# Scores of attention group B as two 128-row products and a set of four 32-row products, with the PSUM banks dealt out by hand and the second projections moved ahead of the output projection

## The chip, the cores and the metric

The kernel runs on one core of a Trainium2 chip. The metric is the time of one execution in microseconds (us) on the device. Three runs of the kernel before gave 1156.81, 1157.28 and 1157.65 us; their median, 1157.28 us, is the time before. The engines are named as in the profile: PE multiplies matrices and writes into PSUM, an accumulator of eight banks of 128 x 512 floats; PEld loads PE's stationary operand; DVE, ACT and POOL work on vectors; SP issues most of the DMAs.

## The reference

The program is two layers of an encoder over 512 tokens of width 1024. Only the first layer's attention matters here. It has two head groups: A, eight heads with grouped keys, and B, eight heads of latent attention. For B:

```python
qb = (rmsnorm(cq, b_q_norm) @ b_w_uq).reshape(b, s, B_HEADS, B_NOPE + B_ROPE)      # 64 + 32
q_nope, q_rope = jnp.split(qb, (B_NOPE,), axis=-1)
q_rope = axial_rope(q_rope, row, col)
kvb = (rmsnorm(ckv, b_kv_norm) @ b_w_ukv).reshape(b, s, B_HEADS, B_NOPE + B_V)
k_nope, vb = jnp.split(kvb, (B_NOPE,), axis=-1)
k_rope = axial_rope(kr[:, :, None, :], row, col)                                   # one for all heads
q_full = jnp.concatenate([q_nope, q_rope], axis=-1)
k_full = jnp.concatenate([k_nope, jnp.broadcast_to(k_rope, (b, s, B_HEADS, B_ROPE))], axis=-1)
ob = block_attention(q_full, k_full, vb, (B_NOPE + B_ROPE) ** -0.5)
mixed = jnp.concatenate([oa.reshape(b, s, -1), ob.reshape(b, s, -1)], axis=-1)
return mixed @ w_out
```

So a score of a B head is a sum over 96 numbers, 64 without rotary positions ("nope") and 32 with them ("rope"); the rope part of the key is the same for all eight heads.

## The kernel before

**Numbers in two parts.** PE multiplies numbers of a shorter type, fp32r, in one pass. Each float is kept as a high part, which is the float rounded to fp32r, and a low part, the rest. A product is then the sum of three passes: high by high, low by high, high by low. A tile of two planes holds both: plane 0 the high part, plane 1 the low part. `split` (L962) makes them: ACT writes plane 0 (L967), DVE subtracts it from the source into plane 1 (L964). `mm3` (L606) is the three passes of a weight product: L607, L608 and L609.

**Attention.** `attend` (L1095) goes through the heads of `all_heads` (L1204): eight of A, then four of B's group 0, then four of group 1. Each head takes four steps, one for each block of 128 queries, so that A has 32 steps and B 32. A step does, in the order of the program:

- `scores`: the passes of the score product into one bank (L1131), two for a head of A, three of 96 rows for a head of B. DVE reads the bank, scales it and finds the row's extreme (L1135, "reduce" below), ACT takes the exponential and its sum (L1137), DVE the reciprocal (L1138), POOL multiplies by it (L1139). This leaves the probabilities `p`.
- `transpose`, for the step three before: four PE transposes into one bank (L1106), from which ACT copies the high part (L1108) and DVE makes the low part (L1109).
- `values`, every second step, for two transposed blocks: eight passes (L1119). After a head's second half, `fold` adds the two halves of the output (ACT L1080, DVE L1083) and, for every second head, splits the pair of heads into a tile of the list `O` (L967, L964).
- `step` (L1211), which calls `fill.run(1.5)`: 1.5 us of other PE work is taken from a queue (`Fill`). A part that must be complete is forced with `fill.until`; its credit is then cut back to nothing.

**What is in the queue.** First the latents of B, then `projB(0)` (L972): `q_part`, `k_part` and `v_part` for the four heads of group 0. At the fourth step of B (n == 35 in `step`) the queue gets one output-projection product for columns 0 to 2 (over A's outputs), then `projB(1)`, then the output-projection products for columns 3 to 5 and 6 to 7. `heads_B(g)` begins with `fill.until(f"v{g}")`. When the last head is through, `fill.until("out")` empties the queue, and the output projection over B's outputs follows in two groups of four columns (L1328 on).

**How a B head's operands come about.** In `q_part`, the 128 columns with m = 2 are the rope parts of four heads: ACT copies the product (L988), `rope` rotates it (DVE L683, POOL L685, DVE L686 and L689), and `split` leaves it in `stg`. The columns with m = 0 and 1 hold two heads' nope parts each. SP copies the second head's half to partitions 0 to 63 of its own tile (L997) and each head's 32 rope rows below (L1000). `k_part` does the same for keys (L1015, L1019, L1021), with the common rope key from `kst` (L912, L913), which `ev_kr` made.

**PSUM.** The eight banks are four kinds of tile with their own turns (L76 to L89): "mm" three banks (projections), "s" two (scores), "t" two (transposes), "o" one (values). A tile can be written when the readers of the tile before it in its bank are through.

**Order.** Only the opening and the second layer run in the order in which they are written. In the attention, a scheduler at build time reorders the instructions of each engine; the engines then run their lists strictly in order and wait for semaphores. SP's list of DMAs is in order too, so that a copy which waits for its source holds up all copies and loads behind it.

Of the kernel before, what the change touches and what calls it, by code (L numbers as in the profile page):

```python
# [35 lines left out]
def encoder_kernel(ctx: ExitStack, tc: tile.TileContext, ins, out, dbg=None):  # L36
# [36 lines left out]
        def free(self):  # L73
            give(self.i)

    def bank(tag, bufs):  # L76
        return ps.tile([P, 512], F32, tag=tag, bufs=bufs, name=nm(tag))

    def mmb():
        return bank("mm", 3)  # L80

    def sbk():
        return bank("s", 2)

    def stb():
        return bank("t", 2)

    def ob():
        return bank("o", 1)  # L89

    def scratch(dt=F32):
        return scp.tile([P, 512], dt, tag="sc", name=nm("sc"))
# [822 lines left out]
    def rotary_load():  # L915
        raw = hold["rawr"] = Slot(F32)
# [55 lines left out]
    def projB(g, last):  # L972
        Q, K, V = (QKV[g][z] for z in "QKV")
        iq = [plan([(0, 384, rows(w_uq, 0, 2)[:, :, 384 * g : 384 * g + 384])], 2, 384, (64, 32), POOL),
              plan([(0, 384, rows(w_uq, 2, 1)[:, :, 384 * g : 384 * g + 384])], 1, 384, (64, 32), POOL)]
        iv = plan([(0, 512, rows(w_ukv, 0, 2)[:, :, 512 * g : 512 * g + 512])], 2, 512, (64, 64), POOL)

        def q_part():
            CQ = [s_.pair() for s_ in cqS]
            banks = three(3)  # L980
            for m in (2, 0, 1):
                for k in range(3):
                    hi, lo = (z[:, k % 2, m * P : (m + 1) * P] for z in weights(iq[k // 2]))
                    mm3(banks[m], hi, lo, CQ[k][:, 0, :], CQ[k][:, 1, :], k == 0, k == 2)
                    yield MM3
                if m == 2:
                    qc = scratch()
                    ACT.activation(qc, banks[2], AF.Copy)  # L988
                    qr = rope(qc, cosB, sinB, sw8)
                    stg = Slot()  # L990
                    split(qr, stg.pair())
                else:

                    Q.extend(Slot() for _ in range(2))
                    qa, qb = Q[2 * m].pair(), Q[2 * m + 1].pair()
                    split(banks[m], qa)
                    SP.dma_start(f32(qb[0:64, :, :]), f32(qa[64:128, :, :]))  # L997
                    for e, q in enumerate((qa, qb)):
                        j = 2 * m + e
                        SP.dma_start(f32(q[64:96, :, :]), f32(stg.pair()[32 * j : 32 * j + 32, :, :]))  # L1000
            stg.free()
            if last:
                for s_ in cqS:
                    s_.free()

        def k_part():
            CK = [s_.pair() for s_ in ckS]
            banks = three(2)
            for m in range(2):
                for k in range(2):  # L1010
                    hi, lo = (z[:, k, m * P : (m + 1) * P] for z in weights(iv))
                    mm3(banks[m], hi, lo, CK[k][:, 0, :], CK[k][:, 1, :], k == 0, k == 1)
                    yield MM3
                kn = scratch()
                DVE.tensor_tensor(kn, banks[m], hold["skvb"].t[:, 0:512], op=ALU.mult)  # L1015
                K.extend(Slot() for _ in range(2))
                ka, kb = K[2 * m].pair(), K[2 * m + 1].pair()
                split(kn, ka)
                SP.dma_start(f32(kb[0:64, :, :]), f32(ka[64:128, :, :]))  # L1019
                for k_ in (ka, kb):  # L1020
                    SP.dma_start(f32(k_[64:96, :, :]), f32(kst.pair()[0:32, :, :]))  # L1021
            if last:
                kst.free()
                hold["skvb"].free()
                rpB.free()

        def v_part():
            CK = [s_.pair() for s_ in ckS]
            sB = hold["sB"]
            hi, lo = weights(iv)  # L1030
            for ip in range(2):
                b = mmb()
                V.append(Slot())
                v = V[ip].t.rearrange("p (i h e) -> p i h e", i=2, h=4)
                for ii in range(2):
# [59 lines left out]
    def attend(heads, step):  # L1095
# [29 lines left out]
                h["after"]()  # L1125

        def scores(h, i):
            s = sbk()
            pl = h["passes"](i)
            for n, (lh, rh) in enumerate(pl):  # L1130
                PE.matmul(s, lh, rh, start=n == 0, stop=n == len(pl) - 1)  # L1131
            h["done"](i)
            t = tiny(4)
            p = pp.tile([P, 512], F32, tag="p", name=nm("p"))
            DVE.tensor_tensor_reduce(p, s, zeros.to_broadcast([P, S]), op0=ALU.add, op1=ALU.min, scale=h["scale"](i),  # L1135
                                     scalar=3e38, accum_out=t[:, 1:2])
            ACT.activation(p, p, AF.Exp, bias=t[:, 1:2], scale=-1.0, accum_out=t[:, 2:3])  # L1137
            DVE.reciprocal(t[:, 3:4], t[:, 2:3])  # L1138
            POOL.tensor_scalar(p, p, t[:, 3:4], 1.0, op0=ALU.mult, op1=ALU.mult)  # L1139
# [12 lines left out]
        for x in late_t:  # L1152
            transpose(*x)
            while late_v:
# [22 lines left out]
    def heads_B(g):  # L1177
# [3 lines left out]
        for j in range(4):  # L1181
            q, k = Q[j].pair(), K[j].pair()

            def passes(i, q=q, k=k):
                ts = slice(i * P, (i + 1) * P)
                return [(q[0:96, 0, ts], k[0:96, 0, :]), (q[0:96, 1, ts], k[0:96, 0, :]),
                        (q[0:96, 0, ts], k[0:96, 1, :])]

            def done(i, j=j):
                if i == 3:  # L1190
# [8 lines left out]
            yield dict(e=j % 2, done=done, after=after, scale=lambda i: hold["scB"][:, i : i + 1], passes=passes,  # L1199
                       vlhs=lambda kt, j=j: vv[kt // 2][:, kt % 2, j, :])  # L1200
# [10 lines left out]
    def step(h, i):  # L1211
# [869 lines left out]
```

## Time and profile before

One execution was profiled. It took 1158.44 us; its span, from the first to the last instruction of the program, is 1156.7 us.

| | |
|---|---|
| median of three runs | 1157.28 us |
| profiled execution, its time | 1158.44 us |
| profiled execution, its span | 1156.7 us |
| first score pass of A and of B (L1131) | at 50.6 us and 143.9 us |
| last score pass of B | at 228.0 us |
| last DVE low part of a transposed block (L1109) | from 235.5 us |

How to read it. In a timeline a row is start, duration, engine, line, operation, tiles, and a count where equal instructions stand together. PE's durations overlap: a pass of 512 columns is shown with 0.39 us, though the next one starts 0.23 us after it, so that costs of PE below are taken from start to start. In a group's row the shape is out<-in, then the count, then total busy time and the mean of one in ns, then the idle time of the engine just before, and what ended it. In a row by windows, each engine has its busy time and, in brackets, its number of instructions.

### The profile page before, as it was taken

The numbers are of one execution on the slowest core, as the hardware profiler recorded it, in microseconds if no ns is written. First come the engines' busy times: TensorE is split into PE (matmuls) and PEld (weight loads), VectorE is DVE, ScalarE is ACT, GpSimd is POOL, SyncE is SP. The second block draws the span as 40 slices with busy tenths as digits, with TensorE's granted clock in tenths as the row PEclk, the third lists the DMA queues.
The fourth block names the chain that finished last, engine by engine and source line by source line (L and its number), as shares of the span: only waits on it lengthen the run. The fifth ranks groups of instructions, "written<-read, shape, count | busy, mean of one in ns | idle before, by whom it ended". The sixth has DMA issues, their size and how long they took to land.

```text
span 1156.7 us, 20518 instructions
## 1 busy us (share of the span) xinstructions
PE 1144.4 (99%) x7348; PEld 1022.1 (88%) x7348; DVE 905.6 (78%) x1576; ACT 668.7 (58%) x1135; POOL 579.5 (50%) x711
## 2 busy tenths in 40 slices
PE   9999999999999999999999999999999999999997
PEld 7787788888899999899988998988889999989996
DVE  6887988888877787978784666667996788698875
ACT  6677777755346668534453555555552666773445
POOL 4366252226688892378402232231388789535730
PEclk9999999999999999999999999999999999999999
DMA  7322415222523335933536574433344233372332
GB/s 234 95 79 71 106 51 142 65 64 80 169 92 96 88 99 140 270 105 101 155 92 164 143 182 127 119 108 119 101 155 128 74 90 94 74 192 70 121 121 73
DMA packets 115349, 134.36 MB, mean 116 GB/s; under 512 B 9795, under 2 KB 96752, under 8 KB 115248
## 3 DMA queue, kind: packets, MB, share of 16 engines
q1 hardware_dynamic: 110896, 120.09, 35.2%
q0 software_dynamic: 4032, 12.60, 5.4%
q8 instruction: 58, 0.95, 0.3%
q14 instruction: 43, 0.35, 0.1%
q10 hardware_dynamic: 320, 0.36, 0.1%
HBM read 110.61 MB, written 6.29 MB: 101 GB/s over the span
## 4 chain that ended last, share of the span: by engine, by line
PE 94%; DVE 2%; DMA 1%; issue 1%; ACT 1%; SPq 0%; POOL 0%; DVEq 0%; ACTq 0%; POOLq 0%
PE mm L607 8%; PE mm L608 8%; PE mm L609 8%; PE mm L451 4%; PE mm L453 4%; PE mm L452 4%; PE t L451 3%; PE t L453 3%; PE t L452 3%; PE s L1131 3%; PE o L1119 3%; PE s L451 2%; PE s L453 2%; PE s L609 2%; PE s L452 2%; PE s L607 2%
## 5 line engine op out<-in xcount | busy, mean ns | idle before, releaser
L364 DVE TENSOR_TENSOR wlo<-a,whi 128x896 fp32r<-128x896 f32 x106 | 131.9, 1248 | 56.1 <-ACT whi L363 55.5
L607 PE MATMUL mm<-a,whi 128*128 128x512 f32 x428 | 173.8, 407 | 0.2
L609 PE MATMUL mm<-a,wlo 128*128 128x512 f32 x428 | 168.9, 396 | 0.0
L608 PE MATMUL mm<-a,whi 128*128 128x512 f32 x428 | 168.9, 395 | 0.0
L363 ACT ACTIVATE whi<-a 128x896 fp32r<-128x896 f32 x106 | 100.6, 949 | 110.7 <-PE s L452 30.3
L223 DVE TENSOR_TENSOR wlo<-raw,whi 128x1024 fp32r<-128x1024 f32 (+4 forms) x97 | 111.8, 1158 | 27.6 <-ACT whi L233 27.1
L233 ACT ACTIVATE whi<-raw 128x1024 fp32r<-128x1024 f32 (+3 forms) x100 | 92.2, 924 | 69.9 <-PE s L608 24.9
L451 PE MATMUL mm<-a,whi 128*128 128x256 f32 x430 | 120.6, 280 | 0.0
L453 PE MATMUL mm<-a,wlo 128*128 128x256 f32 x430 | 120.3, 280 | 0.0
L452 PE MATMUL mm<-a,whi 128*128 128x256 f32 x430 | 120.3, 280 | 0.0
L359 POOL TENSOR_TENSOR a<-a 128x128 f32<-128x128 f32 x104 | 98.6, 948 | 8.2
L363 ACT ACTIVATE whi<-raw 128x896 fp32r<-128x896 f32 x58 | 55.1, 953 | 81.0 <-PE s L452 24.6
L358 POOL TENSOR_TENSOR a<-a 128x256 f32<-128x256 f32 x104 | 92.6, 890 | 8.2
L609 PEld LDWEIGHTS mm<-a,wlo 128*128 128x128 f32 x428 | 80.2, 188 | 18.3
L607 PEld LDWEIGHTS mm<-a,whi 128*128 128x128 f32 x428 | 80.4, 188 | 17.2 <-issue 0.9
L608 PEld LDWEIGHTS mm<-a,whi 128*128 128x128 f32 x428 | 80.7, 189 | 14.9 <-DVE a L964 0.2
L364 DVE TENSOR_TENSOR wlo<-raw,whi 128x896 fp32r<-128x896 f32 x58 | 70.8, 1230 | 26.2 <-ACT whi L363 26.1
L1139 POOL TENSOR_SCALAR p<-p,ti 128x512 f32<-128x512 f32 x64 | 45.5, 712 | 86.3 <-DVE ti L1138 62.9
L1724 POOL TENSOR_SCALAR p<-p,ti 128x256 f32<-128x256 f32 x64 | 35.5, 566 | 105.1 <-DVE ti L1723 92.1
L451 PE MATMUL t<-a,whi 128*128 128x256 f32 x312 | 87.5, 280 | 0.0
L453 PE MATMUL t<-a,wlo 128*128 128x256 f32 x312 | 87.2, 280 | 0.0
L452 PE MATMUL t<-a,whi 128*128 128x256 f32 x312 | 87.2, 280 | 0.0
(436 smaller groups left out, 3577.9 us busy)
## 6 DMA issues: line engine op xcount, KB each, us to landing
a<-in_ffn_w_up_dram SPq DMA_DIRECT2D x102, 256.0 KB, 2.8
raw<-in_ffn_w_down_dram SPq DMA_DIRECT2D x34, 512.0 KB, 4.2
raw<-in_ffn_w_down_dram SPq DMA_DIRECT2D x56, 256.0 KB, 2.7
raw<-in_od_w_qkv_dram SPq DMA_DIRECT2D x64, 128.0 KB, 2.9
raw<-in_ffn_w_up_dram SPq DMA_DIRECT2D x12, 512.0 KB, 3.9
wlo<-in_ffn_w_down_dram POOLq DMA_DIRECT2D x12, 512.0 KB, 6.3
a<-a SPq DMA_DIRECT2D x18, 256.0 KB, 3.3
bx<-a SPq DMA_DIRECT2D x32, 128.0 KB, 5.3
```

Source lines behind the costliest of these rows:

```text
L223: z = lambda: (eng or DVE).tensor_tensor(to, src, f32(high), op=ALU.subtract)
L233: ACT.activation(hi[:, 0:m], raw[:, 0:m], AF.Copy)
L358: held(eng.tensor_tensor(r[:, 4:6], r[:, 2:3].to_broadcast([P, 2, P]), r[:, 0:7:6], op=ALU.add))
L359: held(eng.tensor_tensor(r[:, 7], r[:, 3], r[:, 5], op=ALU.subtract))
L363: ACT.activation(hi[:, 0:896], raw[:, 128:1024], AF.Copy)
L364: DVE.tensor_tensor(lo[:, 0:896], raw[:, 128:1024], f32(hi[:, 0:896]), op=ALU.subtract)
L451: PE.matmul(o, wh, x[:, 0], start=kp == 0 and n in (0, 1, 3, 5), stop=False, skip_group_check=True)
L452: PE.matmul(o, wh, x[:, 1], start=False, stop=False, skip_group_check=True)
L453: PE.matmul(o, wl, x[:, 0], start=False, stop=kp == self.np - 1, skip_group_check=True)
L607: PE.matmul(o, wh, xh, start=first, stop=False)
L608: PE.matmul(o, wh, xl, start=False, stop=False)
L609: PE.matmul(o, wl, xh, start=False, stop=last)
```

## The change

- **Scores of B.** For each head, plane 0 of q is now [nope high; rope high; rope low], plane 0 of k is [nope high; rope-key high; rope-key high], plane 1 of q is [nope low; nope high] and plane 1 of k is [nope high; nope low]. Two passes of 128 rows (plane 0 by plane 0, plane 1 by plane 1) then give everything but rope high by rope-key low, a product of 32 rows. These products of a head's four query blocks are made together, at its first step, into four "s" banks, each from another 32-row strip of partitions (`edge`); the steps' two passes accumulate onto them. Before, a head had 12 passes of 96 rows; now it has 8 of 128 rows and 4 of 32 rows. `tc.keep_in_program_order` keeps the four in their order among the pinned instructions.
- **Copies.** The operands need more SP copies: the rope key is copied to all four strips, `edge` tiles are filled by seven copies a group with the rope rows turned by 0, 32, 64 and 96 partitions, and q and k get their second halves. 24 copies become 72, and the output projection has two weight loads more.
- **PSUM.** Each kind now names its banks. `USUAL` is the dealing of before. From the start of B to the end of the attention `FOUR` holds: "mm" two banks, "s" four, "t" one, "o" one. For the last three transposes "t" gets bank 3 as well.
- **The queue.** `projB(1)` goes into it before the first head of B; the output projection follows at n == 35 in four products of two columns. `q_part` and `k_part` take a bank when they need it, no longer three or two at once.

```diff
+    USUAL = dict(mm=[0, 1, 2], s=[3, 4], t=[5, 6], o=[7])
+    FOUR = dict(mm=[0, 1], s=[2, 3, 4, 5], t=[6], o=[7])
+    layout = [USUAL, dict(mm=0, s=0, t=0, o=0)]
+    def share(banks):
+        layout[:] = [banks, dict(mm=0, s=0, t=0, o=0)]
+    def bank(kind):
+        at = layout[0][kind]
+        n = layout[1][kind] % len(at)
+        layout[1][kind] = n + 1
+        return ps.tile([P, 512], F32, tag=f"b{at[n]}", bufs=1, name=nm(kind))
...
+        SP.dma_start(f32(kp[32:64, :, :]), f32(kp[0:32, :, :]))
+        SP.dma_start(f32(kp[64:128, 1, :]), f32(kp[0:64, 1, :]))
...
                     split(qr, stg.pair())
+                    for i in range(4):
+                        for to, fr, m in ((32 * i, 0, 128 - 32 * i), (0, 128 - 32 * i, 32 * i)):
+                            if m:
+                                SP.dma_start(f32(edge.t[to : to + m, P * i : P * i + P]),
+                                             f32(stg.pair()[fr : fr + m, 0, P * i : P * i + P]))
...
                     SP.dma_start(f32(qb[0:64, :, :]), f32(qa[64:128, :, :]))
+                    SP.dma_start(f32(qb[64:128, 1, :]), f32(qa[64:128, 0, :]))
+                    SP.dma_start(f32(qa[64:128, 1, :]), f32(qa[0:64, 0, :]))
                     for e, q in enumerate((qa, qb)):
                         j = 2 * m + e
-                        SP.dma_start(f32(q[64:96, :, :]), f32(stg.pair()[32 * j : 32 * j + 32, :, :]))
+                        for z in range(2):
+                            SP.dma_start(f32(q[64 + 32 * z : 96 + 32 * z, 0, :]),
+                                         f32(stg.pair()[32 * j : 32 * j + 32, z, :]))
...
-                split(kn, ka)
-                SP.dma_start(f32(kb[0:64, :, :]), f32(ka[64:128, :, :]))
-                for k_ in (ka, kb):
-                    SP.dma_start(f32(k_[64:96, :, :]), f32(kst.pair()[0:32, :, :]))
+                lo = scratch(F32R)
+                ACT.activation(ka[:, 0, :], kn, AF.Copy)
+                DVE.tensor_tensor(lo, kn, f32(ka[:, 0, :]), op=ALU.subtract)
+                for z in range(2):
+                    SP.dma_start(f32(kb[0:64, z, :]), f32(ka[64:128, 0, :]))
+                SP.dma_start(f32(ka[0:64, 1, :]), f32(ka[0:64, 0, :]))
+                for e, k_ in enumerate((ka, kb)):
+                    SP.dma_start(f32(k_[64:128, 0, :]), f32(kst.pair()[0:64, 0, :]))
+                    SP.dma_start(f32(k_[64:128, 1, :]), f32(lo[64 * e : 64 * e + 64, :]))
...
         def scores(h, i):
-            s = sbk()
+            if "edge" in h and i == 0:
+                h["s"] = [sbk() for _ in range(4)]
+                edge = h["edge"]()
+                for n in (3, 0, 1, 2):
+                    tc.keep_in_program_order(PE.matmul(h["s"][n], *edge[n], start=True, stop=False))
+            s = h["s"][i] if "edge" in h else sbk()
...
+        share(dict(FOUR, t=[3, 6]))
         for x in late_t:
...
-                return [(q[0:96, 0, ts], k[0:96, 0, :]), (q[0:96, 1, ts], k[0:96, 0, :]),
-                        (q[0:96, 0, ts], k[0:96, 1, :])]
+                return [(q[:, z, ts], k[:, z, :]) for z in range(2)]
+            def edge(j=j):
+                e = QKV[g]["edge"].t
+                at = [32 * ((i + j) % 4) for i in range(4)]
+                return [(e[a : a + 32, P * i : P * i + P], kst.pair()[a : a + 32, 1, :]) for i, a in enumerate(at)]
...
         yield from heads_A()
+        fill.until("v0")
+        share(FOUR)
+        projB(1, True)
         yield from heads_B(0)
...
-            fill.add(*out_proj(w_out, 0, ok, [0, 1, 2], "out"))
-            projB(1, True)
-            fill.add(*out_proj(w_out, 0, ok, [3, 4, 5], "out"))
-            fill.add(*out_proj(w_out, 0, ok, [6, 7], "out"))
+            for m in (0, 2, 4, 6):
+                fill.add(*out_proj(w_out, 0, ok, [m, m + 1], "out"))
...
     fill.until("out")
+    share(USUAL)
```

More of the change, by code (lines that the diff above doesn't have):

```diff
@@ L74, in free @@
             give(self.i)
-    def bank(tag, bufs):
-        return ps.tile([P, 512], F32, tag=tag, bufs=bufs, name=nm(tag))
+    USUAL = dict(mm=[0, 1, 2], s=[3, 4], t=[5, 6], o=[7])
[8 more added lines that the diff above has]
+        return ps.tile([P, 512], F32, tag=f"b{at[n]}", bufs=1, name=nm(kind))
     def mmb():
-        return bank("mm", 3)
+        return bank("mm")
     def sbk():
-        return bank("s", 2)
+        return bank("s")
     def stb():
-        return bank("t", 2)
+        return bank("t")
     def ob():
-        return bank("o", 1)
+        return bank("o")
     def scratch(dt=F32):
@@ L979, in q_part @@
             CQ = [s_.pair() for s_ in cqS]
-            banks = three(3)
+            banks = {}
             for m in (2, 0, 1):
+                banks[m] = mmb()
                 for k in range(3):
@@ L989, in q_part @@
                     qr = rope(qc, cosB, sinB, sw8)
-                    stg = Slot()
+                    stg, edge = Slot(), Slot()
+                    QKV[g]["edge"] = edge
                     split(qr, stg.pair())
+                    for i in range(4):
[3 more added lines that the diff above has]
+                                             f32(stg.pair()[fr : fr + m, 0, P * i : P * i + P]))
                 else:
@@ L1007, in k_part @@
             CK = [s_.pair() for s_ in ckS]
-            banks = three(2)
+            banks = {}
             for m in range(2):
+                banks[m] = mmb()
                 for k in range(2):
@@ L1017, in k_part @@
                 ka, kb = K[2 * m].pair(), K[2 * m + 1].pair()
-                split(kn, ka)
-                SP.dma_start(f32(kb[0:64, :, :]), f32(ka[64:128, :, :]))
-                for k_ in (ka, kb):
-                    SP.dma_start(f32(k_[64:96, :, :]), f32(kst.pair()[0:32, :, :]))
+                lo = scratch(F32R)
[7 more added lines that the diff above has]
+                    SP.dma_start(f32(k_[64:128, 1, :]), f32(lo[64 * e : 64 * e + 64, :]))
             if last:
-                kst.free()
                 hold["skvb"].free()
@@ L1127, in scores @@
         def scores(h, i):
-            s = sbk()
+            if "edge" in h and i == 0:
[4 more added lines that the diff above has]
+            s = h["s"][i] if "edge" in h else sbk()
             pl = h["passes"](i)
             for n, (lh, rh) in enumerate(pl):
-                PE.matmul(s, lh, rh, start=n == 0, stop=n == len(pl) - 1)
+                PE.matmul(s, lh, rh, start=n == 0 and "edge" not in h, stop=n == len(pl) - 1)
             h["done"](i)
@@ L1197, in after @@
                         s_.free()
-            yield dict(e=j % 2, done=done, after=after, scale=lambda i: hold["scB"][:, i : i + 1], passes=passes,
+                    QKV[g]["edge"].free()
+                    if g:
+                        kst.free()
+            yield dict(e=j % 2, edge=edge, done=done, after=after, scale=lambda i: hold["scB"][:, i : i + 1], passes=passes,
                        vlhs=lambda kt, j=j: vv[kt // 2][:, kt % 2, j, :])
```

## The prediction, made before the change was run

> **What bounds the kernel now.** I read the head of the page first, then its slices and its chain of waits.
>
> ```profile
> span 1156.7 us, 20518 instructions
> PE 1144.4 (99%) x7348; PEld 1022.1 (88%) x7348; DVE 905.6 (78%) x1576; ACT 668.7 (58%) x1135; POOL 579.5 (50%) x711
> PEclk9999999999999999999999999999999999999999
> PE 94%; DVE 2%; DMA 1%; issue 1%; ACT 1%; SPq 0%; POOL 0%; DVEq 0%; ACTq 0%; POOLq 0%
> ```
>
> PE is busy 99% of the span, 94% of the chain lies on it, and its clock is full throughout. An edit counts only by what it takes from PE's queue, or by a wait that it puts into it. The change works in attention B, so next the busy time by windows (PE, PEld, DVE, ACT, POOL).
>
> ```profile
> 116.00:145.00 29.00, 28.15 (x176) 22.99 (x174) 27.48 (x67) 22.45 (x49) 7.24 (x9) 1.00 0.44 103
> 144.00:154.00 10.00, 10.00 (x67) 8.71 (x66) 9.29 (x24) 8.84 (x20) 4.98 (x6) 1.00 0.00 0
> 154.00:194.00 40.00, 39.82 (x237) 33.95 (x236) 35.04 (x77) 27.57 (x59) 15.64 (x20) 1.00 0.44 125
> 194.00:218.00 24.00, 24.00 (x133) 20.00 (x133) 19.96 (x45) 15.84 (x32) 5.87 (x9) 1.00 0.21 56
> 218.00:236.00 18.00, 18.00 (x114) 15.00 (x112) 14.91 (x36) 13.00 (x28) 5.29 (x8) 1.00 0.19 59
> 225.00:230.00 5.00, 5.00 (x33) 4.00 (x31) 4.97 (x12) 4.33 (x10) 1.76 (x3) 1.00 0.03 7
> ```
>
> In B (144 to 236) PE idles 0.18 us; there is almost nothing left to win by less waiting. But DVE stands close behind: 9.29 of 10 us at the start and 4.97 of 5 near the end. Here two banks for "t" let PE run ahead while DVE is late.
>
> Last, the costs of PE from start to start, from its timeline of one step:
>
> ```profile
> 158.74 0.87 PE L1131 MATMUL s<-a,a 96*128 96x512 f32 x3
> 159.45 0.60 PE L1106 MATMUL t<-cst,p 128*128 128x128 f32 x4
> 159.80 1.19 PE L1119 MATMUL o<-a,a 128*128 128x256 f32 x8
> 160.83 0.39 PE L607 MATMUL mm<-a,whi 128*128 128x512 f32 x1
> 161.06 0.39 PE L608 MATMUL mm<-a,whi 128*128 128x512 f32 x1
> ```
>
> A pass of 512 columns costs 0.23 us (160.83 to 161.06; three score passes, 158.74 to 159.45, 0.71, so 0.233 with the other steps), four transposes 0.35 to 0.44 (I take 0.44), eight value passes 1.03 at most, 0.95 where they follow at once.
>
> **The change part by part. E1, the score passes.** A head had 12 passes and gets 8 and a set of four 32-row products: 4 x 0.233 = 0.93 us saved. Rows do not matter by themselves: 96 rows took what 128 rows take. What the set costs the trace does not show; its nearest row is a set of four small products that PE holds in another row arrangement than its neighbours:
>
> ```profile
> 110.05 0.40 PE L609 MATMUL mm<-a,wlo 128*128 128x512 f32 x1
> 110.37 0.41 PE L698 MATMUL t<-cst,sc 2*128 2x2 f32 x4
> 110.71 0.50 PE L607 MATMUL mm<-a,whi 128*128 128x512 f32 x1
> 111.05 0.40 PE L608 MATMUL mm<-a,whi 128*128 128x512 f32 x1
> ...
> L698 PE MATMUL t<-cst,sc 2*128 2x2 f32 x4 | 0.4, 202 | 0.0
> ```
>
> The four small ones take 0.41 us together and 0.20 each (the last row, a group), so they start (0.41 - 0.20) / 3 = 0.07 us apart. From 110.05 to 111.05 are 1.00 us for two passes (0.46) and four such starts (0.28): the other 0.26 us is what going over to them and back costs. The set itself takes 0.23 us if the four run together, 4 x 0.233 = 0.93 if one after another; I take 0.44, one pass of 0.23 after three starts of 0.07, since the four use different rows and different banks and have only their starts in common. Per head: -0.93 + 0.26 + 0.44 = -0.23; over eight heads -1.86. In the built order one set (group 0, second head) has a value pass between its third and fourth product, so one more going over: +0.26. **E1 = -1.6 us**, with bounds -3.3 (0.23 a set) and +2.3 (0.93).
>
> [...]
>
> **E2, the waits that go.** Before B, PE idles 0.85 us (29.00 - 28.15); the one large piece is at 126.93:
>
> ```profile
> 126.93 0.73 PE L1131 MATMUL s<-a,a 128*128 128x512 f32 x2 [0.65 <-DMA a<-sc]
> 126.90 1.18 SPq L1000 DMA_DIRECT2D a<-a  x2
> ```
>
> That is a score of A waiting for its q by DMA. The scheduler's new order puts 18.3 us of PE work ahead of it in place of 15.6 (its instructions by the costs above), which covers 0.65 and some of the rest: **E2 = -1.0**. Bounds: 0 (the copy comes as much later), and -2.5: all of the 0.85 + 0.18 us seen, and some ten short gaps in which a pass is shown with 0.39 us but its successor could start after 0.23, 0.16 each and hidden in busy time.
>
> **E3, the single "t" bank.** This speaks against the change. A set of transposes can start only when DVE has read the set before. How long a bank is taken:
>
> ```profile
> 160.09 0.60 ACT L1108 ACTIVATE a<-t 128x512 fp32r<-128x512 f32 x1 [0.88 <-PE t L1106]
> 160.72 0.69 DVE L1109 TENSOR_TENSOR a<-t,a 128x512 fp32r<-128x512 f32 x1 [0.20 <-ACT a L1108]
> ...
> 153.72 0.60 PE L1106 MATMUL t<-cst,p 128*128 128x128 f32 x4
> 154.67 0.58 ACT L1108 ACTIVATE a<-t 128x512 fp32r<-128x512 f32 x1
> 157.01 0.68 DVE L1109 TENSOR_TENSOR a<-t,a 128x512 fp32r<-128x512 f32 x1
> ```
>
> With ACT and DVE free: 159.45 (above) to 160.72 + 0.69, 1.96 us. Crowded: 153.72 to 157.69, 3.97 us. Against this stands the spacing in the new order: I add up PE's work from one set to the next, by the costs above, for the 30 sets of B before its close. One spacing is 0.55 us (group 1, third head: four transposes and one value pass), fifteen lie between 1.95 and 2.43, thirteen between 2.9 and 3.9. Adding up what is missing, a bank taken for 1.96 us every time costs 1.4 us, all at the one pair; 2.45 us costs 4.8; 2.8 us costs 10.4. What stands ahead of L1109 on DVE:
>
> ```profile
> L1135 DVE CUSTOM_DVE_ANT_0 p<-s,zeros,scB 128x512 f32<-128x512 f32 x32 | 23.7, 742 | 2.0 <-PE s L1131 1.4 <-POOL p L1139 0.3
> L1135 DVE DVE_READ_ACCUMULATOR2_ANT ti<- 128x1 f32 x33 | 2.7, 82 | 0.0
> L1138 DVE RECIPROCAL ti<-ti 128x1 f32<-128x1 f32 x34 | 5.4, 158 | 1.7 <-ACT p L1137 1.4
> L1109 DVE TENSOR_TENSOR a<-t,a 128x512 fp32r<-128x512 f32 x36 | 24.5, 684 | 5.2 <-ACT a L1108 5.1
> L1108 ACT ACTIVATE a<-t 128x512 fp32r<-128x512 f32 x36 | 21.3, 595 | 16.6 <-PE t L1106 16.4
> L1137 ACT ACTIVATE p<-p,ti 128x512 f32<-128x512 f32 x34 | 24.4, 719 | 7.8 <-DVE ti L1135 7.5
> L1137 ACT ACTIVATION_READ_ACCUMULATOR p<-p,ti 128x1 f32 x34 | 6.4, 189 | 0.0
> ```
>
> A reduce and a reciprocal are 0.74 + 0.08 + 0.16 = 0.98 us. PE's order puts about one score between two sets, and whether its reduce comes ahead of L1109 or behind it I can't tell, so I count it for half of the sets, 0.49: 1.96 + 0.49 = 2.45, which I take: 4.8 us. The crowded 3.97 can't hold on average: DVE has 0.98 + 0.68 = 1.67 us a step, and the spacings' mean is 2.71. At the close pair the second set's value pass also waits for L1108, with an exponential (0.72 + 0.19) ahead of it on ACT: +0.9. **E3 = +5.7**, bounds 1.4 and 10.4 (a whole reduce ahead every time, 1.96 + 0.82).
>
> Behind a waiting transpose stand the scores of later steps, so DVE then gets its next reduce late and catches up; that is why a wait does not breed the next. The values read what L1109 writes and wait with it.
>
> **At nothing.** Two more "s" banks, fewer "mm" banks: a pair of projections waits for the add (L1065, 0.68 us) of the pair before, at least 2.2 us of scores, transposes and values lie between; uncovered it costs up to 0.7 a time. The set's first product is for the bank of the head's fourth step and waits for the last reduce of the head before; at least 2.3 us lie between. Copies 24 to 72 and two weight loads: DMAs, behind PE's work; the price if late is the third rival's. The two extra loads bring no more columns of splitting.
>
> **Sum.** -1.6 - 1.0 + 5.7 = +3.1 us: span 1156.7 to 1159.8, the profiled execution's 1158.44 to 1161.5, and, as that execution lay 1.16 above the median, 1157.28 to **1160.4 us**.
>
> **The rivals. First, on the other side: the one bank is enough.** DVE takes L1109 as soon as ACT is through, because PE's scores come in later than DVE clears them. Place: the sets of 1.95 to 2.43. Price: E3 1.4, at the close pair alone; the sum is -1.2, 1156.1 us, and 1154.4 with sets of 0.23. Point: E3 below 2.6 us, a bank taken for about 2.1. For it: ACT is early, as it waited 16.4 us for transposes in B (L1108's row). Against it: DVE is the one that is late, 2.34 us between L1108's start and L1109's at 154.67.
>
> **Second, the four products run one after another**, each waiting for the last as two whole passes do: E1 +2.3 in place of -1.6, 1164.3 us. For it: no row shows two products at once. Against it: the four at 110.37 end within 0.41 us, though these are short.
>
> **Third, the first scores of B come late by DMA.** Group 0's rope copies, which fill `edge` and both q, wait for `stg` (L1000 ran at 126.90, 0.59 us each), and behind them on SP are k's: 22 copies to the first head's last, 13.0 us, to 139.9, then a landing of 2.8:
>
> ```profile
> a<-a SPq DMA_DIRECT2D x19, 128.0 KB, 2.8
> 143.94 0.86 PE L1131 MATMUL s<-a,a 96*128 96x512 f32 x3
> POOL sc L685 <- ACT sc L988: 5.3, 1, 5.3
> L223 POOL TENSOR_TENSOR wlo<-raw,whi 128x512 fp32r<-128x512 f32 x3 | 4.5, 1516 | 3.0 <-ACT whi L243 3.0
> ```
>
> They land at 142.7, 1.2 us ahead of B's first score. A second landing behind it (a k tile's copy waits for copies that it overwrites in part) makes it 145.5, 1.6 late: 1162.0 us. POOL's rotation L685, which waited 5.3 us for its source, gives room, though group 1's weight splits (1.52 each) now come ahead of it.
>
> That the change doesn't do what it says is part of the second rival: a set with a value pass in its middle is no set.
>
> **How the numbers follow.** Forecast 0.45, first rival 0.27, second 0.13, third 0.10, others 0.05. A measurement of this kernel tells about 0.2% (2.3 us) from no change, so faster is below 1155.0 and slower above 1159.6. The forecast itself spans +1 to +6 by the bank's 2.2 to 2.6 us: 0.30 slower, 0.15 same. First rival: 0.17 faster, 0.10 same. Second: 0.11 and 0.02 same; third 0.07 and 0.03 same; others 0.04 faster, 0.01 slower. In sum 0.21 faster, 0.30 same, 0.49 slower. The range, 1154 to 1165, takes in the first rival with quick sets and the second; left out are E1 and E2 both at their low ends and E3 above 8, one in ten each.
>
> **What would show it.** E1: the sets' four starts 0.07 apart and the set and its going over 0.70 us in all. E2: no wait of 0.65 for `a<-sc` around 127. E3: PE's idle time in B up from 0.18 to some 4 us or more, put down to DVE's low part ahead of transposes, most of it at spacings under 2.45 and at the third head of group 1. It is wrong if PE's idle time stays under 2 us (first rival), if the four start 0.23 apart (second), or if the first product of B shows a DMA as its releaser (third).

## The result, and the profile after

The changed kernel takes 1164.24 us (median of four runs, 1164.05 to 1164.64) against 1157.18 us before (median of four): a ratio of 1.006, 95% interval 1.0047 to 1.0072, or 7.1 us more. The forecast was 1160.4 us, range 1154 to 1165. The profiled execution of the changed kernel took 1164.64 us; its span is 1162.9.

From the head of the page of the changed kernel and its chain of waits:

```profile
span 1162.9 us, 20570 instructions
PE 1143.6 (98%) x7348; PEld 1016.7 (87%) x7348; DVE 909.2 (78%) x1578; ACT 668.9 (58%) x1137; POOL 578.8 (50%) x711
PE 90%; DVE 5%; ACT 2%; issue 1%; DMA 1%; SPq 0%; POOL 0%; DVEq 0%; ACTq 0%; POOLq 0%
```

PE's work fell by 0.8 us and the span grew by 6.2: the loss is waits. The chain says for whom: DVE 5% where it had 2%. The busy time by windows (PE, PEld, DVE, ACT, POOL) says where; the last two rows are the changed kernel and the kernel before in a stretch of the second layer, which the diff doesn't touch:

```profile
116.00:145.00 29.00, 26.93 (x163) 21.75 (x162) 27.63 (x68) 21.83 (x49) 13.80 (x16) 1.00 0.54 128
145.00:240.00 95.00, 91.42 (x543) 73.14 (x542) 78.72 (x181) 63.90 (x135) 25.24 (x35) 1.00 0.40 106
600.00:780.00 180.00, 176.61 (x1069) 154.76 (x1068) 116.10 (x319) 93.88 (x219) 47.05 (x88) 1.00 0.53 139
```

```profile
600.00:780.00 180.00, 179.18 (x1082) 157.45 (x1081) 117.19 (x326) 95.98 (x226) 48.67 (x92) 1.00 0.52 138
```

PE's idle time went from 0.85 to 2.07 us in the end of A, from 0.18 to 3.58 in B, and from 0.82 to 3.39 in the second layer. Both kernels issue 7348 matrix instructions, in the same order before attention and, but for two products of the second layer that change places, behind it, so the start of the n-th one can be compared. Starts in us for before; for the others the difference to it (e1, e6, e9, e10 are runs told below):

```
n      before   changed     e1     e6     e9    e10   where
400     81.82     -0.92  -1.09  -0.61  -1.28  -0.93   attention A
1400   260.35     +3.17  +0.10  +3.47  -0.24  -1.05   last output products
1440   268.25     +4.25  +0.10  +4.55  +0.81  -1.02   statistics passed
3800   602.13     +3.69  +0.10  +3.98  +0.22  -1.30   second layer
3900   625.52     +4.78  +1.12  +3.76  +0.17  -1.89
4260   682.71     +5.70  +2.05  +3.67  +0.07  -2.05
4800   766.55     +6.17  +2.90  +3.30  -0.30  -2.21
7340  1147.74     +6.38  +2.88  +3.46  -0.47  -2.63   end
```

So the changed kernel gains 0.9 us in the opening, loses 4.1 up to the end of attention, 1.1 right behind it, and 2.5 between 602 and 767 us; 0.6 comes back between. The 0.9 in the opening I don't count as the change's: it is one wait of 0.79 us at 10.45 us in the profile of before, an execution that lay 1.16 us above its median. Of the runs told below, e2, which deals by release in the opening as before does, starts that product at 9.52 us without a wait, as the changed kernel does at 9.51; e4 and e11 wait there 0.55 and 0.32 us for a load of the program's input. So the wait isn't the dealing's. What made the one in before so long was not settled.

The waits themselves, from PE's timeline of the changed kernel; a bracket has the idle time and what ended it:

```profile
165.69 0.39 PE L1147 MATMUL o<-a,a 128*128 128x256 f32 x1 [0.57 <-ACT a L1136]
...
169.85 0.47 PE L617 MATMUL mm<-a,whi 128*128 128x512 f32 x1 [1.09 <-DVE a L1077]
...
224.44 0.60 PE L1134 MATMUL t<-cst,p 128*128 128x128 f32 x4
225.72 0.38 PE L1147 MATMUL o<-a,a 128*128 128x256 f32 x1 [0.69 <-ACT a L1136]
226.54 0.63 PE L1134 MATMUL t<-cst,p 128*128 128x128 f32 x4 [0.43 <-DVE a L1137]
...
265.17 1.05 PE L638 MATMUL t<-ones,acc 128*128 128x1 f32 x8 [0.78 <-DVE acc L633]
...
628.16 0.47 PE L617 MATMUL mm<-a,whi 128*128 128x512 f32 x1 [0.93 <-DVE ti L1766]
687.17 0.36 PE L1723 MATMUL mm<-whi,a 128*128 128x256 f32 x1 [0.63 <-DVE sc L1682]
763.51 0.47 PE L617 MATMUL mm<-a,whi 128*128 128x512 f32 x1 [0.66 <-DVE sc L1682]
```

The rows at 224 to 227 are the close pair of transposes that the prediction named (L1134, L1136, L1137 and L1147 are L1106, L1108, L1109 and L1119 of before). Of the 3.58 us in B, 1.69 stand ahead of value passes that wait for ACT's high part of a block just transposed (L1136, at 154.81, 165.69, 225.72 and 230.67 us), 1.09 ahead of the product at 169.85, 0.59 ahead of transposes that wait for DVE's low part (L1137, at 210.75 and 226.54) and 0.22 ahead of one that waits for its probabilities (234.88). The last three rows stand in code that the diff leaves alone, except for one thing: where its PSUM banks come from.

### The profile page after: what moved, and what is told of

The parts are those of the page before. It is cut to its first block, busy times and chain, and to the rows that moved or that the text cites. A ratio compares the mean times of both kernels' runs of the same rounds, so it can differ in the third digit from the quotient of the medians.

```text
span 1162.9 us, 20570 instructions
## 1 busy us (share of the span) xinstructions
PE 1143.6 (98%) x7348; PEld 1016.7 (87%) x7348; DVE 909.2 (78%) x1578; ACT 668.9 (58%) x1137; POOL 578.8 (50%) x711
## 4 chain that ended last, share of the span: by engine, by line
PE 90%; DVE 5%; ACT 2%; issue 1%; DMA 1%; SPq 0%; POOL 0%; DVEq 0%; ACTq 0%; POOLq 0%
PE mm L617 8%; PE mm L618 8%; PE mm L619 8%; PE mm L461 4%; PE mm L463 4%; PE mm L462 4%; PE t L461 3%; PE t L463 3%; PE t L462 3%; PE s L461 2%; PE s L462 2%; PE s L463 2%; PE s L617 2%; PE s L619 2%; PE s L618 2%; PE s L1164 2%
## 5 line engine op out<-in xcount | busy, mean ns | idle before, releaser
L233 DVE TENSOR_TENSOR wlo<-raw,whi 128x1024 fp32r<-128x1024 f32 (+4 forms) x99 | 112.4, 1140 | 27.6 <-ACT whi L243 27.2
```

The lines of the kernel that those rows point to most:

```text
L233: z = lambda: (eng or DVE).tensor_tensor(to, src, f32(high), op=ALU.subtract)
```

## The experiments

All times stand beside runs of the kernel before on the same chip; differences below are to those.

### Where the second layer's waits come from

In the lists of instructions the product at 628 us waits for DVE's two pieces of L1682, which read the bank that it is to write:

```profile
627.27 0.75 DVE L1682 SCALAR_TENSOR_TENSOR sc<-mm,rb 128x448 f32<-128x448 f32 x2
```

They end at 628.02, and the product starts 0.14 us later; the products at 687 and 763 us start 0.15 us after their L1682. (The bracket at 628 us names L1766, a reciprocal that DVE began at 627.94.) By the same lists, the pool of before had given that product another bank: of a pair of products, the second was read early and the first late, and the pool gave out the second's bank first. Over a stretch of the second layer before dealt its three banks (3, 4, 5 there) in the order 3 5 4 5 3 5 4 5 3 4 5 4 (e5 below has that order as a list); the counter of `bank` deals 2 3 4 2 3 4, whoever is through.

**e1: the dealing alone.** Before, with the counter and `USUAL` throughout.

```diff
-    def bank(tag, bufs):
-        return ps.tile([P, 512], F32, tag=tag, bufs=bufs, name=nm(tag))
+    def bank(kind):
+        at = layout[0][kind]
+        n = layout[1][kind] % len(at)
+        layout[1][kind] = n + 1
+        return ps.tile([P, 512], F32, tag=f"b{at[n]}", bufs=1, name=nm(kind))
```

> The kernel before, with nothing changed but the dealing of PSUM banks: by a counter, in turn, in the usual shares, for the whole program. Theory: the changed kernel loses some 3 us outside attention B because the counter takes the next bank in turn where the pool took the bank that was let go first; in the second layer a projection then waits for the two DVE pieces that read the tile three products back. This kernel should show the same waits at about 620 to 770 us (0.9, 0.6, 0.2, 0.7 us in the changed kernel) and be 2 to 3 us slower than before, 1159 to 1160.5 us. Rival: dealing in turn and dealing by release come to the same here (all waits of the second layer come from something else, as the order of DMAs): within 0.5 us of before.

1162.01 us against 1157.51: +4.5, ratio 1.004 (1.0025 to 1.0055). PE's timeline of this run:

```profile
624.47 0.47 PE L617 MATMUL mm<-a,whi 128*128 128x512 f32 x1 [0.94 <-DVE ti L1733]
683.50 0.36 PE L1690 MATMUL mm<-whi,a 128*128 128x256 f32 x1 [0.64 <-DVE sc L1649]
760.20 0.47 PE L617 MATMUL mm<-a,whi 128*128 128x512 f32 x1 [0.64 <-DVE sc L1649]
```

The same three waits at the same products, with no other edit. By the table the second layer loses 2.8 us, as expected; the expectation had nothing for the 1.2 us between n = 400 and n = 1400. There the scheduler, given other banks, also ordered the instructions anew. PE's busy time at the end of A in e1:

```profile
116.00:145.00 29.00, 27.39 (x169) 22.49 (x168) 27.26 (x68) 21.51 (x46) 9.07 (x11) 1.00 0.44 111
```

PE idles 1.61 us, where before has 0.85.

**e5 and e6: the order of banks mended in the second layer**, in e1's kernel and in the changed one: from the 61st projection bank on, the order that before's pool gave out, as a list (e6's list has the same order with the banks named from another start).

```diff
+        if kind == "mm":
+            nth[0] += 1
+            if nth[0] > 60:
+                n = int(PICKS[nth[0] - 61])
```

> The run of dealing alone with one thing mended: from the 61st projection bank on (the second layer) the order of banks is a list, the one that the pool of the kernel before gave out. Theory (order of banks is the cause of the second layer's waits): the waits at 624, 683, 728 and 760 us go, 2.8 us of the span; what stays is the opening, where the dealing gained 1.1 us, so 1155.8 to 1157.0 us, at or below before. Rival (the waits come from the semaphores that hand-made names bring, not from which bank is next): they stay, 1161 to 1162 us.

> The changed kernel with the same mend: in the second layer the banks in the order that the pool of the kernel before gave out, all else as changed. Theory: 2.5 to 3 us of the 7 us go, 1161.0 to 1162.0 us; the rest is attention B and the statistics behind it at 265 us. Rival: the second layer's waits are moved, not removed: over 1163.5 us.

e5 took 1158.57 us against 1157.67 (ratio 1.0012, 1.0003 to 1.0021), e6 1161.37 against the same (1.0032, 1.0021 to 1.0044). Both lose the waits; e6 in the window of above:

```profile
600.00:780.00 180.00, 179.10 (x1088) 157.41 (x1087) 117.78 (x323) 95.36 (x222) 47.99 (x90) 1.00 0.54 140
```

PE's idle time there is 0.90 us again. The changed kernel is 3.4 us faster by it (+7.1 to +3.7), e1's 3.6 (+4.5 to +0.9). e5 came out 1.6 us above its expectation, which had counted the opening's 1.1 us as a gain of the dealing. The 0.9 us over before that remain lie ahead of the second layer, where A and B are still dealt in turn: in e5 PE idles 1.77 us from 116 to 145 us, 0.92 more than before. Dealing A and B alone in another order wasn't tried.

**e2: pools by stage**, meant to give the release order to all stages.

```diff
+    def share(banks):
+        if layout[1] is not None:
+            layout[1].close()
+        st = ExitStack()
+        layout[:] = [banks, st, st.enter_context(tc.tile_pool(name=nm("ps"), bufs=1, space=PSUM))]
```

> The changed kernel with the same shares of banks by stage, but dealt by a pool of each stage, which gives out the bank that was let go first; the last three transposes have one bank where they had two. Theory of the dealing: the waits in the second layer go, 2 to 3 us faster than the changed kernel, 1161 to 1162 us, and attention B keeps its loss. Rival (the second layer's waits come from something that the change moved elsewhere): the same as the changed kernel, 1164.2 within 0.7 us, with the waits at the same places.

A miss: 1180.85 us, +23.3 (1.0198, 1.0183 to 1.0213). The windows have both halves of the answer:

```profile
135.00:140.00 5.00, 2.63 (x14) 1.61 (x12) 4.51 (x10) 4.76 (x11) 2.08 (x3) 0.98 0.71 160
140.00:145.00 5.00, 4.37 (x18) 4.07 (x19) 4.61 (x12) 2.26 (x5) 2.52 (x3) 0.50 0.72 166
...
620.00:800.00 180.00, 178.97 (x1089) 157.39 (x1088) 117.80 (x323) 94.98 (x222) 47.97 (x90) 1.00 0.53 141
```

In the second layer PE idles 1.03 us, so there the release order does what the theory says. Around B, where one pool makes way for the next, PE idles up to half of the time, and the granted clock falls to 0.50; as a remedy this is useless. That the change of pools is what holds PE up is read from the place alone.

### What the single bank for transposes costs

**e3: one "t" bank alone.** e1's kernel with `share(dict(USUAL, t=[6]))` from the start of B.

> The kernel before with dealing in turn as in the run of dealing alone, and from the start of attention B on one bank for transposes in place of two; the other one lies idle. Prediction's step: a bank taken for 2.45 us a time costs attention B 4.8 us and 0.9 for the values, so 4 to 6 us over the run of dealing alone. Rival: with three score passes and two score banks DVE keeps up and only the shortest spacings pay, 0.5 to 2 us.

1165.36 us, +7.9 (1.0071, 1.0054 to 1.0087): 3.35 over e1, between the two expectations. By the starts of PE's instructions 1.5 us of it come up in B and 1.35 just ahead of the statistics behind it, most of that in one wait, for the low part of a weight:

```profile
263.87 0.51 PE L619 MATMUL mm<-a,wlo 128*128 128x512 f32 x1 [1.16 <-DVE wlo L233]
```

So in B itself the one bank costs 1.5 us with three passes a score; the 1.16 us are DVE being late, and why e3 has them and e1 not was not tried.

**e7: two for transposes, one for projections.** e6 with another share (and bank 1 also for the last three transposes).

```diff
-    FOUR = dict(mm=[0, 1], s=[2, 3, 4, 5], t=[6], o=[7])
+    FOUR = dict(mm=[0], s=[2, 3, 4, 5], t=[1, 6], o=[7])
```

> As the run before this (second layer mended), and from the start of B two banks for transposes and one for projections, where the change has one and two. Theory (the single transpose bank is what attention B pays for, 3 to 4 us with the statistics behind it): 2 to 4 us faster than that run, 1157.5 to 1159.5 us, if the projections' three passes can stand between others while their one bank is read. Rival (the bank taken from the projections costs as much: 16 output products and 20 others that each wait for a read of about 0.7 us and its way): the same or slower, 1161 to 1165 us, with PE's idle time ahead of projections.

1162.31 us, +4.6 (1.0043, 1.003 to 1.0055), 0.9 slower than e6: the rival. PE's idle time, by windows of e7:

```profile
116.00:145.00 29.00, 25.12 (x156) 20.28 (x155) 27.64 (x67) 21.36 (x47) 14.09 (x16) 1.00 0.55 131
145.00:240.00 95.00, 92.51 (x543) 73.64 (x542) 79.42 (x182) 64.92 (x136) 25.43 (x35) 1.00 0.39 105
```

3.88 us in the end of A and 2.49 in B, where e6 has 2.09 and 3.58: the scheduler's order shifted and the wait moved. The rival has the time right, but not the place: the largest wait, 1.35 us at 138.6 us, stands ahead of a value pass, and 0.80 us in B ahead of the weight products L623.

**e9: a second bank without taking one.** The score bank of a head's first step lies idle from its reduce to the next head's set. Every second block is transposed into it.

```diff
-            tb = stb()
+            tb = ps.tile([P, 512], F32, tag="b2", bufs=1, name=nm("t")) if layout[0] is FOUR and i % 2 == 0 else stb()
```

> The changed kernel with the second layer mended, and in attention B every second block is transposed into the score bank of the head's first step, which lies idle from that step's reduce to the next head's set; projections keep their two banks, so transposes have two in turn without taking one from them. Theory (the single transpose bank costs attention B and the statistics behind it about 3 us): 2 to 3 us faster than the mended kernel's 1161.4, 1158.5 to 1159.5 us, with the wait at 265 us gone. Rival (PE's waits in B come from DVE and ACT being late, whatever the banks, or the next head's set now waits for the low part): 1160.5 us or more.

1158.02 us against 1157.80, ratio 1.0 (0.9991 to 1.0009): 3.5 us less than e6's difference. Its window of B:

```profile
146.00:240.00 94.00, 93.62 (x557) 76.19 (x554) 78.35 (x180) 64.11 (x133) 24.90 (x34) 1.00 0.38 105
```

Idle time is 0.38 us where the changed kernel had 3.58: with a second bank the loss of B goes, the waits of value passes and the one of 1.09 us with it. The scheduler orders PE's list anew with the banks, so the price is that of the bank and of the order that comes with it. One expectation failed: the statistics still wait 0.77 us, so that wait is not the bank's alone.

### The queue

**e4: its order alone.** Before, with `projB(1, True)` ahead of `heads_B(0)` and the output projection in four products of two columns.

> The kernel before with nothing changed but the order of the queue: group 1's projections before the first head of B, the output projection behind it in four products of two columns. The prediction put a gain of 1.0 us here (the wait of 0.65 us at 127 us goes): 1156.3 us. Rival: the changed kernel shows 4.6 us of stalls from 100 to 146 us where before had 2.7, so the earlier projections bring DVE and ACT work forward into a stretch in which DVE is busy 95%, and the move costs 1 to 2 us: 1158.3 to 1159.3 us. If neither, 1157.2 within 0.5, the stalls come from the dealing.

1157.94 us against 1157.51, ratio 1.0003 (0.9994 to 1.0012): neither the gain nor the loss. The end of A, and the wait at 127 us:

```profile
116.00:145.00 29.00, 27.82 (x173) 22.78 (x172) 27.81 (x65) 22.14 (x49) 13.68 (x15) 1.00 0.45 103
...
127.48 1.21 PE L1131 MATMUL s<-a,a 128*128 128x512 f32 x4 [0.39 <-DMA a<-sc]
```

The wait for the DMA is shorter, 0.39 us for 0.65, but there. e1, with the old queue and the dealing in turn, has no wait for a DMA in this stretch. So the queue's order is neither enough to take that wait away nor needed for it.

**e10 and e11: the old place in the new kernel.** e9 and e6 with `projB(1, True)` put back behind the first two columns of the output projection at n == 35.

```diff
-        projB(1, True)
...
-            for m in (0, 2, 4, 6):
+            fill.add(*out_proj(w_out, 0, ok, [0, 1], "out"))
+            projB(1, True)
+            for m in (2, 4, 6):
```

> As the run before this, with group 1's projections put back behind the first two columns of the output projection at the fourth step of B, as in the kernel before. Theory (the early projections bring copies, DVE and ACT work to 115 to 170 us, where the changed kernel loses some 2 us that before doesn't lose): another 1 to 2 us faster, 1157 to 1158 us, at par with before. Rival (as the queue alone showed, its order is worth nothing): within 0.5 us of the run before this.

> The changed kernel with the second layer mended and the old place of group 1's projections, transposes in one bank as changed. If the queue's order costs the changed kernel 1 to 2 us (stalls from 115 to 170 us): 1159.5 to 1160.5 us. If it is worth nothing there: 1161.4 within 0.5 us.

e10 took 1155.89 us against 1157.80, ratio 0.9985 (0.9976 to 0.9994): 2.1 us better than e9 and faster than both kernels. e11 took 1158.83 (1.0011, 1.0002 to 1.0019), 2.7 better than e6. So the early projections cost the changed kernel over 2 us, though e4 shows nothing. By windows of e10 the end of A has part of it:

```profile
116.00:145.00 29.00, 27.77 (x172) 23.05 (x170) 27.75 (x73) 22.42 (x51) 10.64 (x14) 1.00 0.59 143
145.00:240.00 95.00, 94.12 (x560) 76.25 (x560) 82.17 (x182) 66.79 (x137) 28.12 (x37) 1.00 0.38 105
```

1.23 us idle in the end of A against 2.10 in e9 and the changed kernel's 2.07, and no wait left at the statistics (n = 1440 in the table); in B e10 idles 0.88 us, more than e9's 0.38. In e11 the statistics wait no longer either, with one transpose bank. Which of the copies, splits and evacuations that moved makes the difference, and why it needs the new shares of banks, was not tried; nor were the other copies, or the later taking of banks in `q_part` and `k_part`, alone.

### The sets of four

PE's timeline around a set in the changed kernel, and the durations of its products (least, median, most, in ns):

```profile
170.39 0.39 PE L619 MATMUL mm<-a,wlo 128*128 128x512 f32 x1
170.71 0.50 PE L1160 MATMUL s<-a,a 32*128 32x512 f32 x4
171.14 0.73 PE L1164 MATMUL s<-a,a 128*128 128x512 f32 x2
...
L1160 PE MATMUL s<-a,a x32: 489/491/501, 146.0 to 227.9; 32*128 32x512 f32 x32
```

Four products of 0.491 us end within 0.50: they run together, 0.003 us apart. The way in is 0.32 where a pass has 0.23, the set 0.43, and the first pass behind it has 0.34: 0.09 + 0.43 + 0.11 = 0.63 us a set, paid for one that stands between passes of 128 rows.

**e8: all four in one strip of rows.** The changed kernel with `edge` not turned.

```diff
-                        for to, fr, m in ((32 * i, 0, 128 - 32 * i), (0, 128 - 32 * i, 32 * i)):
+                        for to, fr, m in ((0, 0, 128), (0, 128, 0)):
...
-                at = [32 * ((i + j) % 4) for i in range(4)]
+                at = [32 * j for i in range(4)]
```

> The changed kernel with the four 32-row products of a set all in one strip of 32 rows (each head its own), so that no two of a set stand in different rows; same number of products, same banks, 3 copies less for each edge tile. Theory: they ran together in the changed kernel (starts 0.003 us apart, 0.43 us for the four) because of the different rows; in one strip they take 0.23 us each, 0.93 + 0.2 for a set in place of 0.63, and eight sets cost 4 us more: 1167.5 to 1169 us. Rival (they overlap because of the four banks, or because they are short in rows): no change, 1164 within 0.7 us.

1166.27 us, +8.6 (1.0077, 1.0063 to 1.009), only 1.5 over the changed kernel. PE's timeline, the durations of the sets' products and the windows of e8:

```profile
169.69 1.19 PE L1160 MATMUL s<-a,a 32*128 32x512 f32 x4
170.81 0.73 PE L1164 MATMUL s<-a,a 128*128 128x512 f32 x2
...
L1160 PE MATMUL s<-a,a x32: 383/392/500, 146.0 to 230.9; 32*128 32x512 f32 x32
...
145.00:243.00 98.00, 95.98 (x547) 77.27 (x546) 79.76 (x182) 64.70 (x136) 25.07 (x35) 1.00 0.36 99
```

The mechanism is as the theory had it: 1.12 us a set (169.69 to 170.81) in place of 0.43. The price isn't: eight times 0.69 are 5.5 us, and 1.5 were measured. PE's idle time in B falls from 3.58 to 2.02, 1.6 us of the difference: PE, slower, waits less. By the starts of PE's instructions e8 is 2.4 us later than the changed kernel at the end of B, and gains 1.1 back between 606 and 1105 us, where nothing differs by the edit. The one set that a value pass splits in the changed kernel is whole in e8. What takes up the rest is open. A saving on PE in this stretch may be eaten in the same way.

## Why the prediction was right, and where it was wrong

**The direction and the reason** hold: slower, because PE waits in B. **The size** is 7.1 us where 3.1 were forecast, in the upper end of the range. That it equals the second rival's 1164.3 is an accident: the four products run together.

**E1, -1.6 us: right in sum, by two errors that cancel.** Seven whole sets at 0.63 and the one that a value pass splits, 1.4 us without the wait in it, come to 5.8 us of PE for the 7.5 saved. By the prediction's terms the set was 0.44 (measured 0.43) and the going over 0.26 (0.20), which makes eight sets 0.6 us cheaper than counted; the split costs 0.77 more than a whole set, where 0.26 were counted, 0.5 dearer. The 0.44 was also put together wrongly: the starts are 0.003 us apart, not 0.07, and the next pass still comes 0.42 us after the last of them, not 0.23. The first bound (0.23 a set) was too kind for that reason. That the execution becomes 1.6 us faster by it is not shown: no run changes the scores alone.

**E2, -1.0 us: wrong in sign.** The wait of 0.65 us for a DMA at 127 us did go, but the queue's order is neither enough for that (e4 keeps 0.39) nor needed (e1 has none, with the old queue). Other waits came in its place, for DVE: the end of A idles 2.07 us, not 0.85. The failed step is "puts 18.3 us of PE work ahead of it in place of 15.6": it counted PE's work that moved and not what moves with it on DVE, ACT and the copies, in a stretch where DVE was busy 27.48 of 29 us. Dealing in turn has a part in those waits (1.61 us idle in e1, 1.77 in e5, with the old queue), and so has the queue (2.10 in e9, 1.23 in e10). Priced by e9 to e10 and e6 to e11, the queue's order costs 2.1 to 2.7 us; by e4, under the shares of before, nothing.

**E3, +5.7 us: right in kind, over-sized.** From e6 to e9 the single bank costs 3.5 us, from e11 to e10, with the old queue, 2.9; e3 has 3.35 over e1, but only 1.5 of it in B. The step that failed is "which I take", 2.45 us a time. In the changed kernel thirty sets can be followed from their first transpose to the end of L1137: thirteen are at 1.95 to 2.05, the mean is 2.3, and at 2.3 the prediction's own adding up gives 2.9. A reduce stands between L1136 and L1137 in seven of the thirty, not in half of them; in five it is the low part of a weight (L233). The place was wrong as well: of the 3.58 us idle in B only 0.59 stand at transposes that wait for the low part, which the prediction's sign asked for, and 1.69 at value passes behind ACT's high part, which it had for the close pair alone (+0.9; 0.69 there). So that 2.9 lies near the measured price is in part luck.

**At nothing: the step that failed most.** The prediction weighed how many banks each kind gets, and nowhere that a counter deals them in turn where a pool dealt them by release. That is 3.4 us of the 7.1 (changed kernel to e6), all in the second layer, which I never looked at since the diff has no line there; in the end of A the same dealing costs 0.8 to 0.9 us under the shares of before (e1, e5). Of the listed ones, "up to 0.7 a time" for a pair of projections shows once in B: 1.09 us at 169.85, for group 1's values (L1077), not for the add of the output projection. The statistics behind attention weren't thought of: 0.78 us of waiting, 1.1 in the table.

**The third rival** fell: of the waits of PE in B, none is for a DMA.

From the best version to the changed kernel the differences to before go, in this order, from -1.9 (e10) by +2.1 for the queue (e9), +3.5 for the one transpose bank (e6) and +3.4 for the dealing in the second layer to +7.1. The parts depend on the order: by way of e11, the bank is 2.9 and the queue 2.7. e10 has the new scores and is 2.8 us below e5, which has three passes, the old queue and the same list of banks (+0.9). That points the way of E1; as the shares of banks differ too, it is no measure of the scores alone.

## What to carry to other kernels

A change of how buffers are dealt reaches every line that takes one, so look at the stretches that the diff doesn't name, above all where two buffers of a pair are read at different times. Price a single buffer by adding up spacings against the time that it is taken, count in what reads its content next, as the wait may show there, and look for another one that lies idle between its turns before a share is cut. When work is moved earlier, add up what it brings to the engine that is nearly full there, not to the one that bounds.

## What the runs showed of the hardware

The granted clock wasn't full all through these runs: in e2, behind a stretch in which PE was busy 2.63 of 5 us, it was 0.50 for the next 5 us, and two score passes took 1.20 us there in place of 0.73. If the wait is what lowered it, the wait was paid a second time; only the order in time speaks for that:

```profile
138.13 0.73 PE L1166 MATMUL s<-a,a 128*128 128x512 f32 x2 [0.34 <-DVE ti L1170]
143.00 1.20 PE L1166 MATMUL s<-a,a 128*128 128x512 f32 x2
```

The profiled execution of e11, 2.3 us above that kernel's median, has the same order, 0.78 for 5 us behind 5 us in which PE was busy 3.68:

```profile
155.00:160.00 5.00, 3.68 (x18) 2.55 (x17) 3.83 (x11) 3.93 (x10) 1.28 (x2) 0.88 0.00 0
160.00:165.00 5.00, 5.00 (x24) 4.19 (x24) 3.41 (x7) 3.05 (x6) 2.42 (x4) 0.78 0.01 3
```

Four 32-row products of 512 columns took 1.19 us in one strip (e8, at 169.69), one of them 0.392 in the median, so that their starts lie 0.27 us apart on the mean, an estimate from the two; passes of 128 rows start 0.23 apart. In four strips they took 0.50 (changed kernel, at 170.71), and that set cost 0.40 us over a single pass (0.63 less 0.23).
